# A decoder block in one program: lower-part terms last in the first half products, a turning step moved, an output split in front of two merges, the last tile by column halves

## The chip, the cores and the metric

The kernel runs on one core of a Trainium2 chip, and computes the whole block in one launch. The metric is the device time of that launch in microseconds. A run's time is one execution; the time of the kernel is the median of its runs.

## The reference

One decoder layer on 1024 tokens of width 1024, all in float32 (`rms_norm(x, g) = x * rsqrt(mean(x^2) + 1e-6) * g`):

```python
h = x
h = h + 0.5 * swiglu(rms_norm(h, ffn1_norm), ffn1_w1, ffn1_w3, ffn1_w2)   # 1024 -> 2816 -> 1024
u = rms_norm(h, mix_norm)
q, k, v, pz, gate_logits = split(u @ w_in)                 # 768, 768, 768, 512, 2 x 1024 columns
gates = sigmoid(gate_logits)
# 12 heads of 64, in 3 groups of 4 with (window, dilation) = (128,1), (512,4), (2048,16)
y_attn = dilated_mixture_attention(q, k, v) @ w_branch_attn
y_pool = multiscale_pool(pz, pool_w, pool_scale) @ w_branch_pool
merged = gates[:, :, 0] * y_attn + gates[:, :, 1] * y_pool
h = h + merged @ w_out
h = h + 0.5 * swiglu(rms_norm(h, ffn2_norm), ffn2_w1, ffn2_w3, ffn2_w2)
return rms_norm(h, final_norm)
```

In the attention the three groups of a head slot are added with weights that come of their softmax denominators.

## The kernel before

**Products.** Every operand of a large product is split into two parts: an upper part in the matmul's reduced float32 type (ScalarE copies it, names with `hi`) and a lower part, the operand less the upper one (VectorE or GpSimd subtracts, names with `lo`). A product of blocks is then three matmuls: upper by upper, upper by lower, lower by upper. The function `three` lists them in that order. The large products are also made in seven block products instead of eight, on sums and differences of halves; the table `DOWN` says for each of the seven which halves of the result it is added to and with which sign. A matmul writes 128 rows and up to 512 columns of one PSUM bank.

**Order.** The program runs under a manual schedule: each engine works its instructions in the order in which the code issues them, and waits only for what it reads or overwrites. SP issues most transfers, in one queue; ScalarE issues a few.

**The first products.** `run_first(n, ks, terms)` multiplies the first block of the first up-projections: `u_first0` for w1 and `u_first1` for w3, over four slices `k` of the width, with the activations' parts `xhi`, `xlo`. The slices 2 and 3 come later than 0 and 1, since their activations are loaded later; VectorE makes their `xlo`.

**The attention.** `scores(q)`, `masked`, `exponents`, `trans_p` (transposes, `tp`), `split_p` (`ehi` on ScalarE, `elo` on VectorE) and `values(q)` (products `o`) run as a pipeline over `q`, with `house(s)` behind each step for what is due at step `s`, and the pool branch's products `yp` as `fill`. `make_factors` is a generator: each `advance(factors[0])` does its next part. Its third part for the first half of the heads, the turning step, transposes the factors `f` on TensorE (`f_turned`), copies them on ScalarE and stores them (`f_by_head`), and the next part loads them spread over rows (`f_of`). In `house` the parts are advanced at the steps `N // 2 + 8` to `N // 2 + 12`.

**The output product.** `merge(k)` for `k` from 0 to 15 multiplies a column block of the attention branch (six matmuls into a bank, `ya{k}`), multiplies it with the gate on VectorE (`merge{k}`), and adds the pool branch on GpSimd (`merged`). The banks of the tag `mm` are four, so that `ya6` takes that of `ya2`. `sum_o(0)` and `split_o(0)` split the first two blocks of the merged operand: `o_hi0` on ScalarE and `o_lo0` on VectorE, each in two halves. `step_o(0)` then multiplies them with the output weights (`wo`).

**The last product.** `Down.run` ends with a loop over four tiles `t` of 128 rows: the tile's last matmuls (`multiply`, nine of 128x512 into one bank), `add` on VectorE to the residual `h`, and `after2`, which makes the final norm: squares summed on ScalarE (`high_half`), a power on GpSimd (`power`), and `send_out`, in which VectorE scales the upper columns and ScalarE the lower ones and both are stored, 128x512 each. `send_out(3 + t)` of one tile stands behind `high_half` of the next.

## Time and profile before

| | us |
|---|---|
| median of 3 runs | 1876.7 |
| lowest and highest of them | 1875.4, 1876.83 |
| the profiled execution | 1877.42 |
| its span | 1875.2 |
| TensorE busy in the span | 1863.7 (99%) |
| VectorE busy | 1366.2 (73%) |
| GpSimd busy | 783.9 (42%) |
| ScalarE busy | 768.4 (41%) |

The span is what the profile covers, from the first instruction to the end. The granted TensorE clock is 0.999 of full speed over it. TensorE's busy time is nearly the whole span, so the table to read beside it is what TensorE waits for, and what follows its last matmul.

### The profile page before, as it was taken

How to read it: one execution, taken by the hardware profiler on the slowest of the kernel's cores; microseconds unless marked ns; L12 is line 12 of the kernel's file. 1: busy time of each engine (PE TensorE's matmuls, PEld its weight loads, DVE VectorE, ACT ScalarE, POOL GpSimd, SP SyncE). 2: the span in 40 equal slices, each digit the busy share in tenths (PEclk: the TensorE clock that was granted, in tenths of full speed). 3: DMA queues.
4: the chain of work that ended last, by engine and by line, in shares of the span. 5: the costliest groups of instructions: out<-in, count | busy, mean ns of one | idle time of the engine just before them, and what ended most of it. 6: DMA issues, size and time to landing. Idle time of an engine off the chain costs nothing.

```text
span 1875.2 us, 24419 instructions
## 1 busy us (share of the span) xinstructions
PE 1863.7 (99%) x8667; PEld 1545.1 (82%) x8667; DVE 1366.2 (73%) x1966; ACT 768.4 (41%) x1393; POOL 783.9 (42%) x569
## 2 busy tenths in 40 slices
PE   9999999999999999999999999999999999999998
PEld 8888888888888888888888887888888888888886
DVE  7887866668886776658885886887765566577867
ACT  7422323233345643334445772463333333343344
POOL 5554644452222364445554467544333333312221
PEclk9999999999999999999999999999999999999999
DMA  8134324356565436765578888634332233354654
GB/s 327 45 124 149 121 95 152 117 206 209 192 231 198 157 114 208 258 211 185 213 251 324 314 254 298 267 129 180 120 139 85 90 107 122 126 203 157 223 197 146
DMA packets 148369, 339.70 MB, mean 181 GB/s; under 512 B 18024, under 2 KB 39576, under 8 KB 146712
## 3 DMA queue, kind: packets, MB, share of 16 engines
q1 hardware_dynamic: 144504, 327.30, 50.1%
q10 hardware_dynamic: 3744, 10.85, 1.6%
q8 instruction: 68, 1.11, 0.2%
q14 instruction: 53, 0.43, 0.1%
HBM read 237.48 MB, written 100.62 MB: 180 GB/s over the span
## 4 chain that ended last, share of the span: by engine, by line
PE 55%; DVE 2%; ACT 2%; DMA 1%; issue 1%; POOL 1%; SPq 0%; ACTq 0%; POOLq 0%; DVEq 0%
PE u_mixm L334 15%; PE d_f L904 8%; PE wo L2368 4%; PE yp L2110 2%; PE o L2048 1%; PE u_f20a L334 1%; PE u_f20b L334 1%; PE u_f21b L334 1%; PE u_f21a L334 1%; PE u_f210b L334 1%; PE u_f210a L334 1%; PE u_f29b L334 1%; PE u_f29a L334 1%; PE u_f28b L334 1%; PE u_f28a L334 1%; PE u_f27b L334 1%
## 5 line engine op out<-in xcount | busy, mean ns | idle before, releaser
L904 PE MATMUL d_f<-bhi_f,ahi_f 128*128 128x512 f32 x616 | 240.2, 390 | 0.0
L904 PE MATMUL d_f<-bhi_f,alo_f 128*128 128x512 f32 x616 | 239.8, 389 | 0.0
L904 PE MATMUL d_f<-blo_f,ahi_f 128*128 128x512 f32 x616 | 239.7, 389 | 0.0
L861 POOL TENSOR_TENSOR alo_f<-g_f,ahi_f 128x512 fp32r<-128x512 f32 x60 | 86.7, 1462 | 269.0 <-ACT ahi_f L857 269.0
L334 PE MATMUL u_mixm<-xhi_t_mix,wc_mixm 128*128 128x512 f32 x608 | 157.3, 391 | 0.1
L904 PEld LDWEIGHTS d_f<-bhi_f,alo_f 128*128 128x128 f32 x616 | 115.6, 188 | 24.3 <-DVE alo_f L861 0.2
L904 PEld LDWEIGHTS d_f<-bhi_f,ahi_f 128*128 128x128 f32 x616 | 115.6, 188 | 24.1 <-ACT h L424 0.5
L904 PEld LDWEIGHTS d_f<-blo_f,ahi_f 128*128 128x128 f32 x616 | 115.7, 188 | 24.0
L334 PEld LDWEIGHTS u_mixm<-xhi_t_mix,wc_mixm 128*128 128x128 f32 x608 | 113.5, 188 | 23.8 <-ACT wc_mixm L322 0.5
L334 PE MATMUL u_mixm<-xhi_b_mix,wc_mixm 128*128 128x512 f32 x456 | 120.3, 391 | 0.0
L325 POOL TENSOR_TENSOR wc_mixm<-s_mixm,wc_mixm 128x512 fp32r<-128x512 f32 x52 | 77.1, 1483 | 101.8 <-ACT wc_mixm L322 95.7
L334 PEld LDWEIGHTS u_mixm<-xhi_b_mix,wc_mixm 128*128 128x128 f32 x456 | 84.9, 188 | 17.2
L322 ACT ACTIVATE wc_mixm<-s_mixm 128x512 fp32r<-128x512 f32 x76 | 47.0, 628 | 111.4 <-DVE s_mixm L378 56.4
L857 ACT ACTIVATE ahi_f<-g_f 128x1024 fp32r<-128x1024 f32 x84 | 81.9, 975 | 6.8 <-DMA g_f<-gs_f 6.6
L334 PE MATMUL u_mixm<-xlo_t_mix,wc_mixm 128*128 128x512 f32 x304 | 81.3, 389 | 0.0
L325 POOL TENSOR_TENSOR wc_mixm<-raw,wc_mixm 128x512 fp32r<-128x512 f32 x41 | 62.3, 1522 | 37.9 <-ACT wc_mixm L322 24.6
L2368 PE MATMUL wo<-w_o,o_hi 128*128 128x512 f32 x224 | 69.4, 391 | 0.0
L646 POOL TENSOR_TENSOR y_f<-y_f,norm_ffn 128x512 f32<-128x512 f32 x35 | 54.4, 1560 | 35.5 <-DVE y_f L627 25.2
L857 ACT ACTIVATE bhi_f<-s_f2w 128x512 fp32r<-128x512 f32 x55 | 32.9, 627 | 86.0 <-DVE s_f2w L879 69.6
L857 ACT ACTIVATE bhi_f<-s_f1w 128x512 fp32r<-128x512 f32 x55 | 33.1, 629 | 83.5 <-DVE s_f1w L879 70.8
L334 PEld LDWEIGHTS u_mixm<-xlo_t_mix,wc_mixm 128*128 128x128 f32 x304 | 57.1, 188 | 12.0
L861 DVE TENSOR_TENSOR alo_f<-g_f,ahi_f 128x1024 fp32r<-128x1024 f32 (+1 forms) x48 | 58.6, 1222 | 7.7 <-ACT ahi_f L857 7.7
(1360 smaller groups left out, 4823.4 us busy)
## 6 DMA issues: line engine op xcount, KB each, us to landing
g_f<-gs_f SPq DMA_DIRECT2D x70, 512.0 KB
gs_f<-y_f SPq DMA_DIRECT2D x88, 256.0 KB
raw<-in_w2a_dram SPq DMA_DIRECT2D x35, 512.0 KB
raw<-in_w2b_dram SPq DMA_DIRECT2D x35, 512.0 KB
gs_f<-gb_f SPq DMA_DIRECT2D x46, 256.0 KB
raw<-in_w1b_dram SPq DMA_DIRECT2D x22, 512.0 KB
raw<-in_w3b_dram SPq DMA_DIRECT2D x22, 512.0 KB
raw<-in_w1a_dram SPq DMA_DIRECT2D x20, 512.0 KB
```

What stands on the lines that cost most here:

```text
L322: ac.activation(w[:, 0], src, AF.Copy)
L325: eng.tensor_tensor(w[:, 1], src, w[:, 0].bitcast(F32), op=OP.subtract)
L334: pe.matmul(p, a, b, start=(start and n == 0), stop=(n == 11), skip_group_check=not start)
L646: gp.tensor_tensor(c, c, self.sv.norm[:, cols], op=OP.mult)
L857: ac.activation(hi[:, c], src, AF.Copy)
L861: eng.tensor_tensor(lo[:, d], src[:, o], hi[:, d].bitcast(F32), op=OP.subtract)
L904: pe.matmul(self.banks[m][t], l, r, start=(first and q == 0), stop=(last and q == 2))
L2048: pe.matmul(p, l, r, start=(j == 0), stop=(j == end))
L2110: pe.matmul(p, a, b, start=(j == 0), stop=(j == 11))
L2368: pe.matmul(banks[m][t], l, r, start=(st == 0 and j == 0 and q == 0), stop=(st == 1 and j == 1 and q == 2))
```

## The change

Four places in the code are edited.

1. In the first products the slices 2 and 3 of `u_first0` and `u_first1` were each done whole (upper parts, then lower). Now the terms with the activations' upper part are done for both, then those with the lower part for both.
2. The turning step is advanced no longer in `house` but inside step `q`, behind the transposes and the `fill` of that step and in front of `values(q - 2)`.
3. `sum_o(0)` and `split_o(0)` are issued behind `merge(1)` instead of `merge(3)`; `sum_o(1)` stays.
4. The fourth tile of the last product is multiplied, added and squared in two halves of 256 columns. Its first half is issued in `after2` of the third tile. The fourth tile's two sums of squares are added into one on VectorE. The stores of the lower columns of the tiles 5 and 6 go into SP's queue instead of ScalarE's.

```diff
-        def multiply(self, i, t):
+        def multiply(self, i, t, c=slice(0, HALF)):
...
-                for q, (l, r) in enumerate(three(tuple(v[:, j, ts] for v in a), tuple(v[:, j, :] for v in w))):
-                    pe.matmul(self.banks[m][t], l, r, start=(first and q == 0), stop=(last and q == 2))
-
-        def add(self, m, t):
+                for q, (l, r) in enumerate(three(tuple(v[:, j, ts] for v in a), tuple(v[:, j, c] for v in w))):
+                    pe.matmul(self.banks[m][t][:, c], l, r, start=(first and q == 0), stop=(last and q == 2),
+                              skip_group_check=c.start > 0)
...
+        def last_half(self, m, b, part):
+            c, i = (slice(0, HALF // 2), slice(HALF // 2, HALF))[b], len(self.steps) - 1
+            self.multiply(i - 1, 3, c)
+            self.multiply(i, 3, c)
+            self.add(m, 3, c)
+            part(b, c)
...
-                        self.multiply(i - 1, t)
-                        self.multiply(i, t)
-                        self.add(m, t)
+                        if part and t == 3:
+                            self.last_half(m, 1, part)
+                        else:
+                            self.multiply(i - 1, t)
+                            self.multiply(i, t)
+                            self.add(m, t)
                         after(m, t)
...
-        run_first(0, (2, 3), (0, 2, 1))
-        run_first(1, (2, 3), (0, 2, 1))
+        for terms in ((0, 2), (1,)):
+            for n in (0, 1):
+                run_first(n, (2, 3), terms)
...
-        if s - N // 2 in (8, 9, 10, 11, 12):
+        if s - N // 2 in (8, 9, 10, 12):
             advance(factors[0])
...
+                if 2 * q == N // 2 + 12:
+                    advance(factors[0])
             if q > 1:
                 values(q - 2)
...
+            if k == 1:
+                sum_o(0)
+                split_o(0)
             if k == 3:
-                sum_o(0)
                 sum_o(1)
-                split_o(0)
...
+    def last_part(b, c):
+        y, st = ends[7]
+        c = slice(HALF + c.start, HALF + c.stop)
+        ac.activation(y[:, c], h[7][:, c], AF.Square, scale=D ** -0.5, accum_out=st[:, (4, 2)[b]:(5, 3)[b]])
+        if b == 0:
+            ve.tensor_tensor(st[:, 0:1], st[:, 0:1], st[:, 4:5], op=OP.add)
+
     def high_half(t):
+        if t == 7:
+            return
...
-            nc.scalar.dma_start(out[rows, LOWS], y[:, LOWS])
+            (nc.scalar if t == 7 else nc.sync).dma_start(out[rows, LOWS], y[:, LOWS])
...
+            if t == 3:
+                power(7)
             if t > 0:
                 send_out(3 + t)
-            power(4 + t)
+            if t == 2:
+                down.last_half(m, 0, last_part)
+            if t < 3:
+                power(4 + t)
```

**How it moves instructions.** The rows that follow say the line, the operation, what it writes and from what, the shape, and in brackets the engines or queues that it waits for (ending in `_49`, `DMAHW` for transfers); "x2" stands for two alike.

TensorE at the turning step, before: the last value products `o15`, the transposition, and the first scores of the next step.

```order
L2048 MATMUL o15_9731<-ehi15_9690,v4_0_in_9319 128x256
L2048 MATMUL o15_9731<-elo15_9691,v4_0_in_9319 128x256
L2048 MATMUL o15_9731<-ehi15_9690,v4_1_in_9320 128x256
L1917 MATMUL f_turned_9767<-ident_72,f0_9702 48x128 [waits Pool_49]
L1968 MATMUL s18_0_9773<-qk5_1_hi_9429,qk5_0_hi_9426 128x128
L1968 MATMUL s18_1_9774<-qk5_1_hi_9429,qk5_0_hi_9426 128x128 [waits DVE_49]
```

TensorE at the turning step, after: the end of the pool branch's fill `yp10`, the transposition, and the value products `o16` of the next step.

```order
L2122 MATMUL yp10_9722<-xhi_t2_mix_5437,wab5_9489 128x512
L2122 MATMUL yp10_9722<-xlo_t2_mix_5438,wab5_9489 128x512 x3
L1929 MATMUL f_turned_9805<-ident_72,f0_9702 48x128 [waits DVE_49,Pool_49]
L2060 MATMUL o16_9810<-ehi16_9749,v5_0_in_9570 128x256 [waits DMAHW5_49]
L2060 MATMUL o16_9810<-elo16_9750,v5_0_in_9570 128x256
L2060 MATMUL o16_9810<-ehi16_9749,v5_1_in_9571 128x256 [waits DMAHW6_49]
```

The transposition has moved behind a whole step of scores, transposes and fill, in front of `o16`; `o15` and `s18` now follow on each other.

VectorE at the output product's start, before: the last product of the attention (`att`), two merges, the lower parts of the first split, two merges.

```order
L2091 TENSOR_TENSOR att1_1_10274<-o1_2_9869,att1_0_10273 128x512 [waits Activation_49]
L2178 TENSOR_TENSOR merge2_10277<-merge2_10277,ya2_10404 128x512 [waits DMAHW4_49,DMAHW2_49,PE_49]
L2178 TENSOR_TENSOR merge3_10308<-merge3_10308,ya3_10418 128x512 [waits DMAHW5_49,PE_49]
L2356 TENSOR_TENSOR o_lo0_10431<-merged0_0_10387,o_hi0_10430 128x512 [waits Activation_49] x2
L2178 TENSOR_TENSOR merge4_10311<-merge4_10311,ya4_10438 128x512 [waits DMAHW7_49,PE_49]
L2178 TENSOR_TENSOR merge5_10389<-merge5_10389,ya5_10453 128x512 [waits DMAHW4_49,DMAHW1_49,PE_49]
```

VectorE at the same place, after.

```order
L2103 TENSOR_TENSOR att1_1_10274<-o1_2_9869,att1_0_10273 128x512 [waits Activation_49]
L2370 TENSOR_TENSOR o_lo0_10405<-merged0_0_10387,o_hi0_10404 128x512 [waits Activation_49] x2
L2190 TENSOR_TENSOR merge2_10277<-merge2_10277,ya2_10410 128x512 [waits DMAHW4_49,DMAHW2_49,PE_49]
L2190 TENSOR_TENSOR merge3_10308<-merge3_10308,ya3_10424 128x512 [waits DMAHW5_49,PE_49]
L2190 TENSOR_TENSOR merge4_10311<-merge4_10311,ya4_10438 128x512 [waits DMAHW7_49,PE_49]
L2190 TENSOR_TENSOR merge5_10389<-merge5_10389,ya5_10453 128x512 [waits DMAHW4_49,DMAHW1_49,PE_49]
```

The two `o_lo0` have moved in front of `merge2` and `merge3`.

VectorE in the tail, before: the additions of the third and fourth tile (`h6_last`, `h7_last`), the statistics (`nst`) and the scalings (`n4`).

```order
L912 SCALAR_TENSOR_TENSOR h6_last_14054<-d_f26_2_15994,h6_last_14054 128x512 [waits PE_49]
L2560 SCALAR_TENSOR_TENSOR n4_5_16081<-h5_last_14052,nst_last5_16082,gain_final_14058 128x512 [waits Pool_49]
L2554 SCALAR_TENSOR_TENSOR nst_last6_16127<-nst_last6_16127 128x1 [waits Activation_49]
L912 SCALAR_TENSOR_TENSOR h7_last_14056<-d_f26_3_15995,h7_last_14056 128x512 [waits PE_49]
L2560 SCALAR_TENSOR_TENSOR n4_6_16126<-h6_last_14054,nst_last6_16127,gain_final_14058 128x512 [waits Pool_49]
L2554 SCALAR_TENSOR_TENSOR nst_last7_16168<-nst_last7_16168 128x1 [waits Activation_49]
L2560 SCALAR_TENSOR_TENSOR n4_7_16167<-h7_last_14056,nst_last7_16168,gain_final_14058 128x512 [waits Pool_49]
```

VectorE in the tail, after.

```order
L913 SCALAR_TENSOR_TENSOR h6_last_14054<-d_f26_2_15994,h6_last_14054 128x512 [waits PE_49]
L2584 SCALAR_TENSOR_TENSOR n4_5_16081<-h5_last_14052,nst_last5_16082,gain_final_14058 128x512 [waits Pool_49]
L913 SCALAR_TENSOR_TENSOR h7_last_14056<-d_f26_3_15995,h7_last_14056 128x256 [waits PE_49]
L2568 TENSOR_TENSOR nst_last7_16168<-nst_last7_16168 128x1 [waits Activation_49]
L2578 SCALAR_TENSOR_TENSOR nst_last6_16127<-nst_last6_16127 128x1
L913 SCALAR_TENSOR_TENSOR h7_last_14056<-d_f26_3_15995,h7_last_14056 128x256 [waits PE_49]
L2578 SCALAR_TENSOR_TENSOR nst_last7_16168<-nst_last7_16168 128x1 [waits Activation_49]
L2584 SCALAR_TENSOR_TENSOR n4_6_16126<-h6_last_14054,nst_last6_16127,gain_final_14058 128x512 [waits Pool_49]
L2584 SCALAR_TENSOR_TENSOR n4_7_16167<-h7_last_14056,nst_last7_16168,gain_final_14058 128x512 [waits Pool_49]
```

The addition of the fourth tile is two of 256 columns, its first stands in front of the third tile's statistics, and the scaling of `n4_6` has moved behind the second. On TensorE the nine last matmuls are now eighteen of 256 columns, of which the tenth waits for VectorE, as the rows around it show:

```order
L904 MATMUL d_f26_3_15995<-bhi_f240_16114,alo_f240_16121 128x256
L904 MATMUL d_f26_3_15995<-bhi_f241_16157,ahi_f241_16161 128x256
L904 MATMUL d_f26_3_15995<-blo_f241_16158,ahi_f241_16161 128x256
L904 MATMUL d_f26_3_15995<-bhi_f241_16157,alo_f241_16162 128x256
L904 MATMUL d_f26_3_15995<-bhi_f240_16114,ahi_f240_16120 128x256 [waits DVE_49]
L904 MATMUL d_f26_3_15995<-blo_f240_16115,ahi_f240_16120 128x256
L904 MATMUL d_f26_3_15995<-bhi_f240_16114,alo_f240_16121 128x256
```

What has moved there: the second half of the columns starts anew with the first weights, in the same bank.

## Rows read from the trace of the kernel before

**Rows 1.** Busy times by stretch: us, busy us of each engine (x instructions), TensorE clock.

```profile
1866.00:1875.20 9.20, 2.27 (x11) 1.54 (x9) 4.43 (x9) 3.39 (x7) 2.09 (x3) 0.74 0.62 228
...
sum 1875.20, PE 1863.74 PEld 1545.12 DVE 1366.21 ACT 768.36 POOL 783.90; mean PE 931.87 PEld 772.56 DVE 683.10 ACT 384.18 POOL 391.95
```

**Rows 2.** Timeline of TensorE, first products: start, us, instruction, [idle before <- releaser].

```profile
10.38 0.39 PE L1158 MATMUL u_first<-xlo_b_f,wc_first 128*128 128x512 f32 x1
11.75 0.50 PE L1158 MATMUL u_first<-xlo_b_f,wc_first 128*128 128x512 f32 x1 [0.98 <-DVE xlo_b_f L1066]
12.09 1.10 PE L1158 MATMUL u_first<-xhi_b_f,wc_first 128*128 128x512 f32 x4
13.03 0.62 PE L1158 MATMUL u_first<-xlo_b_f,wc_first 128*128 128x512 f32 x2
```

**Rows 3.** Timeline of GpSimd, first products.

```profile
6.25 3.12 POOL L1148 TENSOR_TENSOR wc_first<-raw,wc_first 128x256 fp32r<-128x256 f32 x4 [5.81 <-ACT wc_first L1144]
```

**Rows 4.** Timeline of TensorE around the turning step.

```profile
1095.18 0.28 PE L2048 MATMUL o<-elo,v_in 128*128 128x256 f32 x1
1095.30 0.28 PE L2048 MATMUL o<-ehi,v_in 128*128 128x256 f32 x1
1096.20 0.29 PE L1917 MATMUL f_turned<-ident,f 128*48 128x128 f32 x1 [0.62 <-POOL f L1912]
1096.43 0.33 PE L1968 MATMUL s<-qk_hi,qk_hi 64*128 64x128 f32 x2
...
1099.33 0.28 PE L2048 MATMUL o<-ehi,v_in 128*128 128x256 f32 x1
...
1100.96 1.26 PE L2015 MATMUL tp<-ident,e 128*128 128x128 f32 x4
```

**Rows 5.** Timeline of ScalarE around the turning step.

```profile
1096.53 0.27 ACT L1919 ACTIVATE f_turned<-f_turned 48x128 f32<-48x128 f32 x1 [1.70 <-PE f_turned L1917]
1098.67 0.60 ACT L2027 ACTIVATE ehi<-tp 128x512 fp32r<-128x512 f32 x1 [1.86 <-PE tp L2015]
1099.16 1.15 ACT L1590 ACTIVATE xlo_b_mix<-xhi_b_mix 128x512 fp32r<-128x512 f32 x2
```

**Rows 6.** Timeline of VectorE at the output product's start.

```profile
1138.90 0.68 DVE L2178 TENSOR_TENSOR merge<-merge,ya 128x512 f32<-128x512 f32 x1
1141.65 0.69 DVE L2178 TENSOR_TENSOR merge<-merge,ya 128x512 f32<-128x512 f32 x1 [2.08 <-DMA merge<-gate]
1142.26 2.37 DVE L2356 TENSOR_TENSOR o_lo<-merged,o_hi 128x512 fp32r<-128x512 f32 x2
```

**Rows 7.** Timelines of TensorE, ScalarE and GpSimd at the output product's start.

```profile
1139.17 3.34 PE L2176 MATMUL ya<-att,ya 128*128 128x512 f32 x14
...
1144.68 0.50 PE L2368 MATMUL wo<-w_o,o_lo 128*128 128x512 f32 x1 [0.72 <-DVE o_lo L2356]
...
1145.02 0.64 PE L2368 MATMUL wo<-w_o,o_hi 128*128 128x512 f32 x2
...
1140.16 0.63 ACT L2355 ACTIVATE o_hi<-merged 128x512 fp32r<-128x512 f32 x1 [1.07 <-POOL merged L2182]
...
1136.62 4.75 POOL L2182 TENSOR_TENSOR merged<-merge 128x512 f32<-128x512 f32 x3
```

**Rows 8.** Timeline of the tail, from the last matmuls to the last store.

```profile
1867.24 0.74 DVE L2560 SCALAR_TENSOR_TENSOR n<-h_last,nst_last,gain_final 128x512 f32<-128x512 f32 x1
...
1867.89 0.39 PE L904 MATMUL d_f<-bhi_f,alo_f 128*128 128x512 f32 x1
...
1868.31 0.69 DVE L912 SCALAR_TENSOR_TENSOR h_last<-d_f,h_last 128x512 f32<-128x512 f32 x1
...
1871.62 0.34 ACTq L2565 DMA_DIRECT2D out_dram<-n  x1
```

**Rows 9.** Groups of instructions by line and form: busy us, mean ns of one.

```profile
L2030 DVE TENSOR_TENSOR elo<-tp,ehi 128x256 fp32r<-128x256 f32 x10 | 4.2, 422 | 1.8 <-ACT ehi L2027 1.7
```

**Rows 10.** Transfers from 1871.6 us on, GB/s in 40 slices of 0.09 us.

```profile
GB/s 387 410 432 364 251 69 0 114 319 410 364 364 387 364 364 364 364 387 364 410 387 432 341 92 0 0 0 0 0 0 0 0 0 0 0 0 0 0 0 0
```

More of the change, by code (lines that the diff above doesn't have):

```diff
@@ L902, in multiply, with add @@
                 first, last = s == 0 and j == 0, s == len(PAIRS) - 1 and j == size - 1
-                for q, (l, r) in enumerate(three(tuple(v[:, j, ts] for v in a), tuple(v[:, j, :] for v in w))):
-                    pe.matmul(self.banks[m][t], l, r, start=(first and q == 0), stop=(last and q == 2))
-        def add(self, m, t):
+                for q, (l, r) in enumerate(three(tuple(v[:, j, ts] for v in a), tuple(v[:, j, c] for v in w))):
+                    pe.matmul(self.banks[m][t][:, c], l, r, start=(first and q == 0), stop=(last and q == 2),
+                              skip_group_check=c.start > 0)
+        def add(self, m, t, c=slice(0, HALF)):
             for (th, n), sign in DOWN[m].to:
-                hs = h[4 * th + t][:, n * HALF:(n + 1) * HALF]
+                hs = h[4 * th + t][:, n * HALF + c.start:n * HALF + c.stop]
                 by = 0.5 * sign
@@ L911, in add, with run @@
                     by = self.halves[sign][:, 4 * th + t:4 * th + t + 1]
-                ve.scalar_tensor_tensor(hs, self.banks[m][t], by, hs, op0=OP.mult, op1=OP.add)
-        def run(self, pool, after, tick=None):
+                ve.scalar_tensor_tensor(hs, self.banks[m][t][:, c], by, hs, op0=OP.mult, op1=OP.add)
+        def last_half(self, m, b, part):
[4 more added lines that the diff above has]
+            part(b, c)
+        def run(self, pool, after, tick=None, part=None):
             def half_tile(tag, n):
@@ L1157, in run_first @@
                     a, b = three((w[:, 0, r], w[:, 1, r]), (hi[:, k, :], lo[:, k, :]))[i]
-                    pe.matmul(banks[n], a, b, start=(k == 0 and i == 0), stop=(k == 3 and i == terms[-1]))
+                    pe.matmul(banks[n], a, b, start=(k == 0 and i == 0), stop=(k == 3 and i == 1))
         FRONT, BACK = slice(0, 2 * P), slice(2 * P, HALF)
@@ L2535, in low_half @@
     def low_half(t):
-        y, st = h_tile(f"n4_{t}"), small.tile([P, 4], F32, tag="nlast", name=f"nst_last{t}")
+        y, st = h_tile(f"n4_{t}"), small.tile([P, 5], F32, tag="nlast", name=f"nst_last{t}")
         ac.activation(y[:, LOWS], h[t][:, LOWS], AF.Square, scale=D ** -0.5, accum_out=st[:, 0:1])
@@ L2594, in tile_block @@
         with tc.manual_schedule():
-            down.run(pool, after2)
+            down.run(pool, after2, part=last_part)
     dstack.close()
```

## The prediction

> **What bounds the kernel now.** I read the busy times by stretch first. TensorE works 1863.7 of 1875.2 us [rows 1], so all that it waits for comes to 11.5 us, and 6.9 of these lie behind its last matmul, from 1866 us on, where it works 2.27 of 9.20 us. No edit can be worth more than the waits that it touches. 0.2% of the time, which is about what a measurement of this kernel can tell from no change, is 3.75 us. The list of waits by engine then says which line waits for whom, and timelines of four places give the rest; in those, a wait stands in brackets behind the row. The four edits touch four places, in order of time: a 0.98 us wait of TensorE for VectorE at 11.75 [rows 2]; a 0.62 us wait for GpSimd at 1096.20 [rows 4]; a 0.72 us wait for VectorE at 1144.68 [rows 7]; and the tail, in which no matmul is left and the time is that of one chain through VectorE, ScalarE, GpSimd and a store [rows 8]. The profiled execution took 1877.42 us, 2.2 more than its span, and 0.72 more than the median of the three runs, 1876.7. I make the sum as a difference and put it on the median.
>
> **Lower-part terms last.** TensorE has done the four upper-part matmuls of `u_first0` and starts its lower-part one at 10.38; the next needs a part that VectorE finishes only at 11.75. Behind it stand `u_first1`'s four upper-part matmuls at 12.09, which need nothing late: their rows show no wait [rows 2], and GpSimd has split the last of their weights by 6.25 + 3.12 = 9.37 [rows 3]. The change puts these four into the gap. They take 13.03 - 12.09 = 0.94, so they fill 10.38 to 11.32; the first lower-part matmul takes until about 11.55, the second still waits for 11.75, and all behind it comes 0.94 earlier: **-0.94**. What is left of the gap is 0.2. Bounds: -1.05 if the slow restart (the matmul at 11.75 takes 0.34 to the next, not 0.23) goes too, and 0 if a later wait for an operand swallows all. After that, up to the middle of the program, the list of waits has for TensorE none as long as this one; I take -0.94.
>
> **Turning step moved.** Before, TensorE starts its last `o15` matmul at 1095.30, the transposition `f_turned` waits for GpSimd until 1096.20, and the scores `s18` start at 1096.43. A matmul of 256 columns takes 0.12 to the next (1095.18 to 1095.30), so without the step the scores start at about 1095.42: 1.01 earlier [rows 4]. The step itself comes behind the fills, in front of `o16`, which stood at 1099.33, so at about 1098.32; GpSimd is long done by then. But the change leaves ScalarE's order alone: its copy of `f_turned` still stands in front of `ehi17`. The copy started 0.33 after the transposition, so now at 1098.65, and takes 0.27; `ehi17`, at 1098.67 before, starts at about 1098.89, and ScalarE then works without a pause through two splits and four exponentials [rows 5], which `tp18` on TensorE waits for: four matmuls from 1100.96 take 1.26 [rows 4]. So TensorE gains 1.01 and gives it back at `tp18`, where it is ScalarE's 0.22 that counts: **+0.2**. Bounds: -0.9 if ScalarE's lateness does not reach `tp18`; +0.9 if the step's two transfers, on SP's queue now behind the store of `by_pool4` and 2.1 us later (copy at 1098.65, not 1096.53), hold up the factors that GpSimd and VectorE multiply with. In the waits of this stretch TensorE waits for nothing that comes of those factors before the branch products, 30 us on, so I take the ScalarE number.
>
> **First split in front of two merges.** Before, VectorE does `merge2` at 1138.90, waits for a load until 1141.65, does `merge3`, and only at 1142.26 the two `o_lo` of the first split, 2.37 for both [rows 6]: 0.69 for one, as `merge3` shows for the size, and 1.7 for the other. TensorE waits for it at 1144.68 for 0.72, and goes on with its seventh `wo` matmul at 1145.02 [rows 7]. A matmul of 512 columns takes (3.34 - 0.39) / 13 = 0.227 (the 14 of `ya`), so this is as if `wo` had started at 1145.02 - 6 x 0.227 = 1143.66 without a wait. After, the first `o_lo` goes while GpSimd makes the second of its additions (three take it from 1136.62 to 1141.37 now; ScalarE's second `o_hi` waits for the second until 1140.16). The second `o_lo` comes behind that `o_hi`, 1140.16 + 0.63 = 1140.79, and takes 0.69, to 1141.48: GpSimd's third addition needs `merge2`, and so stands still then. Then comes `merge2`, until 1142.15 and not 1139.58. That is a new wait: `ya6` takes the bank that `merge2` reads, and would have started at 1139.17 + 8 x 0.227 = 1140.98. It starts at 1142.2, its six matmuls end at 1143.6, and `wo` then runs without a wait: 1143.6 against 1143.66, **-0.05**. Bounds: -1.1 if `ya6` is not held, and +1.0 if the second `o_lo` takes the 1.7 us that it takes now. `merge3` waits for its load until 1141.65 either way.
>
> **Last tile by halves.** Nine matmuls of 512 columns become eighteen of 256. The order shows a wait on VectorE at the first matmul of the second half: the addition of the first half reads the bank that the second half writes. The nine used to start at 1867.89 - 8 x 0.227 = 1866.07. Now half 0 ends at 1866.07 + 8 x 0.12 + 0.28 = 1867.31. Its addition finds VectorE in a row of 0.74 from 1867.24, so it starts at 1867.9 [rows 8], takes 0.42 (the one row type of 256 columns out of PSUM: 422 ns [rows 9]) and ends at 1868.32. Half 1 runs from 1868.37 to 1869.61, its addition starts at 1869.65. Before, the whole addition started at 1868.31. So 1.34 is lost, and the shorter addition (0.69 to 0.42) and a square shortened as much give 0.5 back: the last store would be issued +0.84 later, at 1872.46. That isn't all: `n4_6`'s scaling now stands behind the second addition and its statistics, so that four stores of 256 KB go out within a us, not two. In the last stretch bytes flow from 1872.2 to 1873.76 for two stores (17 slices of 0.09), 0.75 each, starting 0.6 behind the issue at 1871.62, and the span ends 1.44 later [rows 8, 10]. Four, the first issued at about 1871.5, flow from 1872.1 to 1875.1: 1.35 later than 1873.76, **+1.4** rounded up for the issues. Bounds: +0.84 if the stores cost nothing more, and +2.2 if additions and squares of half the width cost as much as whole ones and the stores come in addition. A bound below nothing belongs to the rival without the wait.
>
> The Trainium skill, "PSUM — Partial Sum Buffer", section "PSUM bank collisions raise a hardware error", says that two engines on one bank collide even at disjoint columns, and that the compiler makes any two such instructions depend on each other. By it the wait is there and the last edit is a loss, and without it that term would be -0.45; no row of before shows a bank shared by halves, and the order prints the wait. The same skill, "SBUF — State Buffer", section "The DMA setup-cost knee", gives a transfer 2 us and its bytes at 436 GB/s, by which I estimate two more stores of 256 KB at +1.2 instead of 1.4.
>
> **Sum.** -0.94 + 0.2 - 0.05 + 1.4 = +0.6, so 1876.7 + 0.6 = **1877.3**: no change that can be measured.
>
> **Rivals.** (1) *Each edit does what it removes.* -1.05, -0.9, -1.1, and in the tail a second half that does not wait: it ends at 1868.3 as before, and the shorter addition and square give -0.45. Together -3.5: 1873.2. For it speaks that each wait is in the trace, against it that rows 5 and 6 show what stands behind each of the last three. (2) *The stores at the end pile up*, the other side. Four stores drain together. At the 228 GB/s that the last stretch had on average [rows 1] the megabyte takes 4.6 us, so bytes flow until 1876.7, +2.9, and the sum gives 1878.8. Over +0.2% it comes below 170 GB/s (6.2 us: +4.5). Against it: the last slices show 341 to 432 GB/s. (3) *The early gain is swallowed* by a later wait for an operand that ScalarE or GpSimd makes at their own pace: 0 for the first edit, 1878.2.
>
> **How the numbers follow.** I give the forecast 0.6, rival 1 0.15, rival 2 0.13, rival 3 0.12. The likeliest's own range has the tail between +0.84 and +2.2 and half the spread of the three runs (1.4) either way: 1876.0 to 1878.8. To hold 8 in 10 the range goes down to 1874.5, where the first three edits do what rival 1 says and the tail loses its least (-3.05 + 0.84 = -2.2), and up to 1880.2: rival 2 with the upper bound of the turning step (+0.7) and half the spread. Faster by over 0.2% needs more than all of rival 1, and holds 0.06. Slower by over 0.2% needs rival 2 at its point or several upper bounds: 0.08. The rest, 0.86, is within 0.2%.
>
> **What would show it.** Right: TensorE reaches `u_f11a` at about 12.55; `f_turned` stands without a wait near 1098.3 and `tp18` comes no earlier than before against the rows around it; `ya6` has a wait for `merge2` of about 1.2, and `wo` none for `o_lo`; a gap of about 1 us in front of the tenth of the last eighteen matmuls, and four stores in the last 4 us. Wrong: no gap at the tenth matmul or at `ya6` (then it is faster than said, by 1.3 each at most), or the 0.94 of the start gone by 60 us.

## The result, and the profile after

| | median us | runs | lowest to highest |
|---|---|---|---|
| before | 1876.71 | 20 | 1875.4 to 1879.13 |
| after | 1880.12 | 20 | 1879.15 to 1881.37 |

The ratio is 1.0017, with a 95% interval from 1.0011 to 1.0024: the change costs 3.4 us, and between 2.1 and 4.5 by the interval. The time lies inside the range, by 0.1, and inside 0.2% (3.75 us), 2.8 above the forecast time. The interval lies above 1, so there is a change, and its upper end lies past 0.2% and past the range. The profiled execution took 1880.36 us with a span of 1878.1.

The waits of TensorE in the changed kernel (engine, line, what it waited for: us in total, times, longest):

```profile
PE fa L1958 <- ACT f_of L1949: 1.1, 1, 1.1
PE idle L1052 <- DVE fours L1053: 1.1, 1, 1.1
PE ya L2188 <- DVE merge L2190: 1.0, 1, 1.0
PE d_f L904 <- DVE h_last L913: 1.0, 1, 1.0
PE tp L2027 <- ACT e L2007: 0.8, 2, 0.6
PE d_f L904 <- POOL alo_f L861: 0.5, 1, 0.5
```

Of the three waits on which the prediction was built, those for `xlo` [rows 2], `f` [rows 4] and `o_lo` [rows 7], none is left. Four of 0.5 to 1.1 us stand in their place: `fa`, `ya`, the `d_f` for VectorE and that for GpSimd. The third and fourth line, `ya` and `d_f <- h_last`, were forecast with about their sizes (1.2 and 1). The first was not forecast. The line of `tp`, of which 0.6 is the wait at `tp18`, was.

The last stretch, which answers to [rows 1]:

```profile
1866.00:1878.10 12.10, 4.10 (x26) 3.42 (x24) 5.79 (x13) 4.31 (x11) 2.83 (x4) 0.78 0.47 173
```

TensorE works 4.10 of its 12.10 us, not 2.27 of 9.20: the end of the third tile and the eighteen matmuls, with a wait between them. TensorE at the start, which answers to [rows 2]:

```profile
9.66 1.87 PE L1169 MATMUL u_first<-xhi_b_f,wc_first 128*128 128x512 f32 x7
11.37 1.07 PE L1169 MATMUL u_first<-xlo_b_f,wc_first 128*128 128x512 f32 x4
12.27 1.07 PE L334 MATMUL u_f11a<-xhi_b_f,wc_f11a 128*128 128x512 f32 x4
```

The seven upper-part and four lower-part matmuls run without a gap. The four lower-part ones run from 11.37 on, where [rows 2] had the last two at 13.03, and `u_f11a` behind them starts at 12.27; before it started at 13.49. From the last tile's first matmul to the end of the span it was 1875.2 - 1866.07 = 9.1; now it is 1878.1 - 1867.53 = 10.6.

The turning step and what hangs on it, in the order of the chain, after (TensorE's rows at the step first, then SP's queue, GpSimd, ScalarE, TensorE):

```profile
1098.28 0.28 PE L1929 MATMUL f_turned<-ident,f 128*48 128x128 f32 x1
1100.83 1.48 PE L2027 MATMUL tp<-ident,e 128*128 128x128 f32 x4 [0.63 <-ACT e L2007]
...
1098.89 0.33 SPq L1932 DMA_DIRECT2D f_by_head<-f_turned  x1
...
1107.50 2.55 POOL L2093 TENSOR_TENSOR o<-o,f_of 128x512 f32<-128x512 f32 x2 [1.43 <-DMA f_of<-f_by_head]
...
1122.60 0.63 ACT L2102 ACTIVATE att<-o 128x512 fp32r<-128x512 f32 x1 [1.55 <-POOL o L2097]
1126.21 2.00 ACT L1949 ACTIVATE f_of<-f 128x1024 f32<-128x1024 f32 x2 [1.87 <-DVE f L1924]
...
1127.32 0.66 PE L1958 MATMUL fa<-ident,f_of 128*128 128x128 f32 x4 [1.06 <-ACT f_of L1949]
```

The store of the factors starts at 1098.89, not 1096.83. GpSimd's first product with the loaded factors comes at 1107.50 and waits 1.43 for their load; before it had no wait. GpSimd's products and sums follow on each other from there with one short pause, and ScalarE's copy `att` of the second round of them waits 1.55 for GpSimd at 1122.60; behind it in ScalarE's order stand two `ehi`, the exponent of the other half's factors, and at 1126.21 the copies that spread them (`f_of`). TensorE's transpositions `fa` of these wait until 1127.32. The first two rows show the step itself as it was forecast: no wait at 1098.28, and 0.63 for ScalarE at `tp18`. In the kernel before GpSimd, `att` and `fa` had no wait in the same chain:

```profile
1096.83 0.33 SPq L1920 DMA_DIRECT2D f_by_head<-f_turned  x1
...
1105.94 2.56 POOL L2081 TENSOR_TENSOR o<-o,f_of 128x512 f32<-128x512 f32 x2
...
1121.06 0.63 ACT L2090 ACTIVATE att<-o 128x512 fp32r<-128x512 f32 x1
1124.69 2.00 ACT L1937 ACTIVATE f_of<-f 128x1024 f32<-128x1024 f32 x2 [1.89 <-DVE f L1912]
...
1126.03 0.60 PE L1946 MATMUL fa<-ident,f_of 128*128 128x128 f32 x4
```

The output product, TensorE and VectorE, and the tail, in the timelines of after (answering to [rows 6, 7, 8]):

```profile
1143.68 1.66 PE L2188 MATMUL ya<-att,ya 128*128 128x512 f32 x6 [1.04 <-DVE merge L2190]
1145.17 0.62 PE L2382 MATMUL wo<-w_o,o_hi 128*128 128x512 f32 x2
...
1140.64 2.39 DVE L2370 TENSOR_TENSOR o_lo<-merged,o_hi 128x512 fp32r<-128x512 f32 x2
1142.94 2.56 DVE L2190 TENSOR_TENSOR merge<-merge,ya 128x512 f32<-128x512 f32 x4
...
1867.53 0.28 PE L904 MATMUL d_f<-bhi_f,ahi_f 128*128 128x256 f32 x1
...
1869.28 0.42 DVE L913 SCALAR_TENSOR_TENSOR h_last<-d_f,h_last 128x256 f32<-128x256 f32 x1
...
1869.75 0.39 PE L904 MATMUL d_f<-bhi_f,ahi_f 128*128 128x256 f32 x1 [0.99 <-DVE h_last L913]
...
1871.13 0.42 DVE L913 SCALAR_TENSOR_TENSOR h_last<-d_f,h_last 128x256 f32<-128x256 f32 x1 [0.39 <-PE d_f L904]
...
1874.14 0.37 ACTq L2589 DMA_DIRECT2D out_dram<-n  x1
```

`ya6` waits 1.04 for `merge2`, which starts at 1142.94 behind the two `o_lo`, and `wo` then runs without a wait. In the tail the first half's addition starts at 1869.28, the tenth matmul waits 0.99 for it, and the last issue on ScalarE's queue comes at 1874.14, 6.6 behind the tile's first matmul; before it was 5.55 (1866.07 to 1871.62).

Laid side by side, the two traces say where the 2.9 us between their spans come from. TensorE in the changed kernel is 1.2 ahead at `u_f11a` (12.27 against 13.49), 0.1 ahead at the last `o15` (1095.16 against 1095.30), 1.3 behind at `fa` (1127.32 against 1126.03), 1.5 behind from the output product to the last tile (1867.53 against 1866.07) and 2.9 behind at the end. So the start's gain is lost before the turning step, the turning step costs 1.4 up to `fa`, the split next to nothing and the tail 1.4. Each trace is one execution.

### The profile page after: what moved, and what is told of

Its sections match the earlier page's. It is cut to its first block, busy times and chain, and to the rows that moved or that the text cites. A ratio compares the mean times of both kernels' runs of the same rounds, so it can differ in the third digit from the quotient of the medians.

```text
span 1878.1 us, 24443 instructions
## 1 busy us (share of the span) xinstructions
PE 1864.4 (99%) x8676; PEld 1545.2 (82%) x8676; DVE 1368.2 (73%) x1968; ACT 768.1 (41%) x1395; POOL 783.1 (42%) x569
## 4 chain that ended last, share of the span: by engine, by line
PE 53%; DVE 2%; ACT 2%; POOL 1%; issue 1%; DMA 1%; SPq 0%; POOLq 0%; ACTq 0%; DVEq 0%
PE u_mixm L334 15%; PE d_f L904 8%; PE wo L2382 4%; PE yp L2122 1%; PE u_f20a L334 1%; PE u_f21b L334 1%; PE u_f20b L334 1%; PE u_f21a L334 1%; PE u_f210b L334 1%; PE u_f210a L334 1%; PE u_f29b L334 1%; PE u_f29a L334 1%; PE u_f28b L334 1%; PE u_f28a L334 1%; PE u_f27b L334 1%
```

## The experiments

Each kernel was timed against the kernel before on the same chip, 11 runs of it and 33 of before. The differences are of medians, the intervals those of the ratio, each about 1.7 us wide to either side. Nothing is left out of the computation in any of them.

| kernel | us against before | ratio, 95% interval |
|---|---|---|
| a_only | -0.36 | 0.9999 (0.9990 to 1.0008) |
| b_only | +1.03 | 1.0007 (0.9998 to 1.0016) |
| c_only | -0.05 | 1.0001 (0.9992 to 1.0010) |
| d_only | +1.66 | 1.0009 (1.0001 to 1.0018) |
| b_swap | +4.13 | 1.0023 (1.0014 to 1.0032) |
| late_store | +2.17 | 1.0014 (1.0005 to 1.0023) |
| b_early | +2.12 | 1.0010 (1.0001 to 1.0018) |
| c_two | -0.46 | 0.9997 (0.9988 to 1.0006) |
| d_bank | +0.55 | 1.0005 (0.9996 to 1.0013) |
| d_acts | +1.21 | 1.0009 (1.0000 to 1.0017) |
| a_c_two | -0.12 | 0.9997 (0.9988 to 1.0006) |
| best | +0.52 | 1.0002 (0.9993 to 1.0011) |

**Each edit alone.** The kernel before with one edit of the diff above.

> The kernel before with the first edit alone (lower-part terms last in the first half products). Theory 1, from the trace after the change: TensorE is 0.9 to 1.2 us ahead from 13 us on, but at about 464 us it waits for GpSimd's lower part of a reloaded operand, whose transfer does not come earlier by as much, and at 760 us for ScalarE once more; some 0.2 is left at 1090 us, so the time is -0.2 (within +-0.6) against before. Theory 2, the prediction: nothing swallows it, -0.94. The start itself should show no wait of 0.98 for the lower part under either.

> The kernel before with the second edit alone (turning step moved). Theory 1: the step's late transfers cost, not its place on TensorE: the loads of the factors start some 2.1 us later, the row statistics of the other half of the heads, behind them in SP's queue, land some 2 us later, VectorE waits for them near 1121, and TensorE waits about 1.1 us for the spread factors at its transpositions near 1126: +1.4 to +1.6 in all, with the 0.2 of ScalarE at tp18. Theory 2, the prediction: only ScalarE's 0.2 at tp18 counts: +0.2. Theory 3: the stall near 1126 comes of another edit in front of it (the first one's shift); then it is absent here and the time is +0.2 too, with no wait of VectorE for the statistics.

> The kernel before with the third edit alone (first split in front of two merges). Theory 1 and the prediction: the wait moves from the wo matmuls to ya6, which is held by about 1.2 us for merge2, and the net is 0 (-0.1 to +0.1). Rival: ya6 is held in the changed kernel because all there is 1.5 us late; alone the edit gains the 1.1 us of the two waits for o_lo, -1.1.

> The kernel before with the fourth edit alone (last tile by column halves, two stores moved to the other queue). Theory 1 and the prediction: TensorE stands about 1 us in front of the tenth of the eighteen last matmuls, the last store is issued 0.9 to 1.1 later against the first matmul of the last tile, and the time is +1.4 (1.2 to 1.7). Rival: the loss belongs to what came in late from the edits in front, and alone the halves cost nothing or gain: 0 to -0.45.

The four add up to +2.3, under the +3.4 of all together but within its interval (2.1 to 4.5); whether the 1.1 between them is more than the spread stays open. By these intervals only the fourth edit is told from 0, and it costs; that the second costs too rests on its trace and on the kernels that follow. The first is worth little and the third nothing that could be measured.

*The first edit.* The 0.98 us that it takes away is not in every execution. Each kernel's trace is one execution. Of the ten traces of kernels without the edit, the list of waits has TensorE waiting for VectorE's `xlo` in five, but in two of these at another place:

| before | b_only | c_two | b_early | d_acts | c_only, d_only, b_swap, late_store, d_bank |
|---|---|---|---|---|---|
| 1.0 | 1.1 | 1.0 | 0.7 | 0.7 | none |

The 0.7 of `b_early` and `d_acts` stands in front of the first two slices, which the edit leaves alone; at the slices 2 and 3 these traces have no wait:

```profile
7.95 0.50 PE L1158 MATMUL u_first<-xlo_b_f,wc_first 128*128 128x512 f32 x1 [0.65 <-DVE xlo_b_f L1066]
```

So the wait of [rows 2] is there in three traces of ten, which is 0.31 in the mean, and -0.36 is what the edit alone gave. VectorE and GpSimd show why, first in the kernel before, then in `a_only`, whose edit does not touch their order, and in `c_only`; the second row of the first two is the second lower part alone:

```profile
8.68 3.01 DVE L1066 SCALAR_TENSOR_TENSOR xlo_b_f<-x_t,gain,xhi_b_f 128x512 fp32r<-128x512 f32 x2 [2.00 <-ACT xhi_b_f L1057]
...
9.84 1.85 DVE L1066 SCALAR_TENSOR_TENSOR xlo_b_f<-x_t,gain,xhi_b_f 128x512 fp32r<-128x512 f32 x1
...
9.86 1.28 POOL L325 TENSOR_TENSOR wc_f11a<-raw,wc_f11a 128x512 fp32r<-128x512 f32 x1 [0.49 <-ACT wc_f11a L322]
```

```profile
8.88 1.79 DVE L1066 SCALAR_TENSOR_TENSOR xlo_b_f<-x_t,gain,xhi_b_f 128x512 fp32r<-128x512 f32 x2 [1.41 <-ACT xhi_b_f L1057]
...
9.93 0.74 DVE L1066 SCALAR_TENSOR_TENSOR xlo_b_f<-x_t,gain,xhi_b_f 128x512 fp32r<-128x512 f32 x1
...
10.06 1.77 POOL L325 TENSOR_TENSOR wc_f11a<-raw,wc_f11a 128x512 fp32r<-128x512 f32 x1 [0.59 <-ACT wc_f11a L322]
```

```profile
8.59 1.84 DVE L1066 SCALAR_TENSOR_TENSOR xlo_b_f<-x_t,gain,xhi_b_f 128x512 fp32r<-128x512 f32 x2 [1.37 <-ACT xhi_b_f L1057]
```

Two lower parts took VectorE 1.79 and 1.84 where the second of them started ahead of GpSimd's subtraction, and 3.01 in the kernel before, where the second one took 1.85 and not 0.74; there GpSimd's took 1.28, and in `a_only` 1.77. The ten traces without the edit fall apart in the same way. In the three with the wait GpSimd's subtraction took 1.28 to 1.33 and VectorE's 1.77 to 1.85; in the seven others, GpSimd's took 1.74 to 1.83 and VectorE's 0.74 or 1.23. In these seven VectorE started 0.06 to 0.64 us ahead; in `b_only` and `c_two` GpSimd was 0.1 ahead (9.87 against 9.97, 10.27 against 10.38), and in the kernel before the two starts lie 0.02 apart (9.84 and 9.86). Which of the two is stretched hangs on a tenth or less. The Trainium skill, "SBUF — State Buffer", section "SBUF: two separate sides", says that a VectorE operation with two inputs in SBUF and a GpSimd operation that reads SBUF take one pair of ports as an exclusive lock, whoever starts first for the whole instruction; the nine traces with starts at least 0.06 apart agree, and that of the kernel before cannot tell who was first.

In the profile of the changed kernel the early gain was mostly gone by the turning step: the last `o15` came at 1095.16, 0.14 ahead of [rows 4], after a new wait of 0.5 for GpSimd's `alo_f` at 464 us and smaller losses near 727 and 760 us. In the traces of `a_only` and `c_only` a start that was earlier by a us stayed so up to the output product, so swallowing it is not the rule; this part of the first theory fell.

*The second edit.* `b_only` shows the chain again, with a wait for the statistics that was expected:

```profile
1099.24 0.33 SPq L1920 DMA_DIRECT2D f_by_head<-f_turned  x1
...
1107.92 2.55 POOL L2081 TENSOR_TENSOR o<-o,f_of 128x512 f32<-128x512 f32 x2 [1.50 <-DMA f_of<-f_by_head]
...
1123.02 0.63 ACT L2090 ACTIVATE att<-o 128x512 fp32r<-128x512 f32 x1 [1.62 <-POOL o L2085]
...
1122.86 0.17 DVE L1903 TENSOR_TENSOR top<-top,stats 128x16 f32<-128x16 f32 x1 [1.22 <-DMA stats<-st]
...
1127.75 0.66 PE L1946 MATMUL fa<-ident,f_of 128*128 128x128 f32 x4 [1.14 <-ACT f_of L1937]
```

VectorE waits 1.22 for the statistics at 1122.86, but what VectorE makes of them goes to ScalarE's exponent, which stands behind `att` and two `ehi`, so this trace does not yet tell which of the two sets the end. The next two kernels do.

**The transfers or the place.** `late_store` leaves the transposition and its copy where they were, and makes the transfers late, at the price of a second small copy on ScalarE:

```diff
             ac.activation(turned, p, AF.Copy)
-            nc.sync.dma_start(f_dram.rearrange("g a i p -> (g a i) p"), turned)
+            yield
+            again = att_small.tile([GROUPS * 2 * NT, P], F32, name="f_turned_again")
+            ac.activation(again, turned, AF.Copy)
+            nc.sync.dma_start(f_dram.rearrange("g a i p -> (g a i) p"), again)
...
                 advance(splits[q - 1], 2)
+            if 2 * q == N // 2 + 12:
+                advance(factors[0])
```

> The kernel before, in which the turning step stays where it was on TensorE and ScalarE, but what is stored is a second copy, which ScalarE makes behind ehi17, so that the store and the four loads of the factors start some 2.6 us later (2.1 in the changed kernel). Theory 1 (late transfers): VectorE waits for the statistics near 1121 and TensorE for the spread factors near 1126, 1.1 to 1.7 us, with the f_turned wait of 0.6 still there: +1.2 to +1.8. Rival (place): the cost of the second edit is what the step does at its new place on TensorE and ScalarE; then this costs only the copy, +0.3 or less.

It cost 2.17, with the transposition at its old place: late transfers cost by themselves. In its trace GpSimd waits 2.75 for the factors and `fa` 1.24, and the eight `tp` in front of that take 1.91, before 1.04:

```profile
1095.33 0.29 PE L1917 MATMUL f_turned<-ident,f 128*48 128x128 f32 x1 [0.62 <-POOL f L1912]
...
1108.05 2.55 POOL L2084 TENSOR_TENSOR o<-o,f_of 128x512 f32<-128x512 f32 x2 [2.75 <-DMA f_of<-f_by_head]
...
1116.76 1.91 PE L2018 MATMUL tp<-ident,e 128*128 128x128 f32 x8
...
1127.84 0.66 PE L1949 MATMUL fa<-ident,f_of 128*128 128x128 f32 x4 [1.24 <-ACT f_of L1940]
```

It does not match the second edit in size. Its loads are issued 6.6 us behind the last `o15` (1094.43 to 1101.04), in `b_only` 5.2 (1095.51 to 1100.71), in the kernel before 3.0 (1095.30 to 1098.31), so they are later than the edit makes them; that goes with the larger cost.

`b_swap` puts what stands behind the factors' loads in SP's queue in front of them:

```diff
-        if s - N // 2 in (8, 9, 10, 12):
+        if s - N // 2 in (8, 9, 10):
             advance(factors[0])
         if i == 4 and u + 1 < len(uses):
             load_values(uses[u + 1])
         if u > 0 and i == 4 and slots[s - 5][1] != 0:
             get_stats(*slots[s - 5][:2])
+        if s - N // 2 == 12:
+            advance(factors[0])
```

> The second edit alone, with one thing more: in SP's queue the loads of the next values and the statistics of the other half of the heads stand in front of the four loads of the factors, so that they fill the time in which the transfers wait for the late turning step (about 5 us without a byte in the changed kernel's trace, 1097.2 to 1102.2). Theory 1 (late transfers): the statistics come back to where they were or earlier, VectorE's wait for them near 1121 and TensorE's 1.1 us at the transpositions near 1126 go, and +0.2 of ScalarE at tp18 is left: +0.0 to +0.3 against before, some 1 us under the edit alone. Rival: the lateness comes of the factors themselves, not of what is queued behind them; then GpSimd, which needs them near 1106, is later still by some 2 us, and the time is +1.0 or more.

It cost 4.13, four times the edit alone. So the theory that the statistics behind the loads set the end fell: with them out of the way the loads of the factors themselves came later, and GpSimd waited 3.75 for them:

```profile
1109.38 1.30 POOL L2081 TENSOR_TENSOR o<-o,f_of 128x512 f32<-128x512 f32 x1 [3.75 <-DMA f_of<-f_by_head]
...
1118.09 1.91 PE L2015 MATMUL tp<-ident,e 128*128 128x128 f32 x8 [1.05 <-ACT e L1995]
...
1129.18 0.66 PE L1946 MATMUL fa<-ident,f_of 128*128 128x128 f32 x4 [1.25 <-ACT f_of L1937]
```

ScalarE's `att` waits for GpSimd, and since its exponents for the attention stand behind it, `tp` waits too, 1.05, and then `fa`, 1.25. The chain is: store of the turned factors, their load, GpSimd's products, ScalarE in order, `fa`.

**The step one place earlier.** `b_early` advances the step behind `scores(q + 1)` in place of behind the fill:

```diff
                 scores(q)
                 scores(q + 1)
+            if 2 * q == N // 2 + 12:
+                advance(factors[0])
```

> The second edit with the turning step one place earlier: behind the scores s18 and s19, in front of the transposes tp17, where GpSimd's factors are there and ScalarE is idle. Theory 2 (chain of the factors): the loads are there 8.7 us after the store starts (1099.24 to 1107.92 in the kernel with the second edit alone), GpSimd then multiplies, ScalarE copies and makes the exponent of the other half's factors behind that, and TensorE's transpositions near 1126 come at the end with 0.2 to spare before. The store is some 0.7 later than before, so GpSimd starts some 0.2 later, and what TensorE gains at 1096 it gives back near 1126: 0.0 (-0.3 to +0.4). Rival (wait on TensorE): the 0.6 wait was worth something, nothing here is late enough to count: -0.6 to -0.9.

```profile
1097.21 0.27 PE L1917 MATMUL f_turned<-ident,f 128*48 128x128 f32 x1 [0.72 <-DVE own_stats L1986]
...
1106.38 2.55 POOL L2081 TENSOR_TENSOR o<-o,f_of 128x512 f32<-128x512 f32 x2 [1.05 <-DMA f_of<-f_by_head]
...
1126.23 0.66 PE L1946 MATMUL fa<-ident,f_of 128*128 128x128 f32 x4 [0.70 <-ACT f_of L1937]
```

The forecast of a store 0.7 later was wrong: the transposition takes a bank of the four that the scores use, and waited 0.72 for VectorE to read it. The load came late here too, GpSimd waited 1.05 and `fa` 0.70. The time, +2.12, is more than these waits explain in this trace, whose execution at 1876.99 was one of the fastest three of its kernel; the rest stays open. Neither place that was tried behind the old one gained.

**The split one merge later.** As the third edit, with `if k == 2` for `if k == 1`.

> The third edit alone with the split one merge later, behind merge(2): VectorE does merge2, both lower parts, merge3. Theory: what holds ya6 is merge2 behind the lower parts; with merge2 in front, ya6 starts with no wait near its 1140.98 of before, the lower parts end by about 1142, before wo needs them, and the time is -0.9 to -1.2 against executions with the whole o_lo wait, -0.4 to -0.8 on the median, since that wait was short in some executions. Rival: merge3, now behind the lower parts, holds the next product's bank and the wait only moves on: 0.

```profile
1138.67 5.15 PE L2176 MATMUL ya<-att,ya 128*128 128x512 f32 x22
1143.65 0.62 PE L2368 MATMUL wo<-w_o,o_hi 128*128 128x512 f32 x2
1144.11 0.39 PE L2368 MATMUL wo<-w_o,o_lo 128*128 128x512 f32 x1
```

The 22 `ya` matmuls and `wo` run through without a wait, in 5.15 us: neither `ya6` nor `wo` is held, which the theory said and the rival denied. (`fa` waits 0.4 in this trace, though the turning step is at its old place.) The gain of -0.46 has 0 in its interval.

The 0.72 of [rows 7] is a sample too. Of the nine traces with the split behind `merge(3)`, the list has a wait for `o_lo` in three (0.7 in the kernel before, 0.2 in `b_only`, 1.0 in two waits in `late_store`) and none in six, while `ya6` waits 1.04 in both traces with the split behind `merge(1)`. By these traces the third edit should lose that us against an execution without the old wait; why the median of `c_only` shows no loss stays open.

**The halves of the last tile.** In `d_bank` the second half goes into a bank of its own; the first addition takes the whole first bank, and the sums of squares are added behind the second one:

```diff
-                    pe.matmul(self.banks[m][t][:, c], l, r, start=(first and q == 0), stop=(last and q == 2),
-                              skip_group_check=c.start > 0)
+                    p = self.rest if c.start > 0 else self.banks[m][t]
+                    begin = c.start > 0 and i == len(self.steps) - 2 and j == 0
+                    end = self.name == "f2" and t == 3 and i == len(self.steps) - 3 and j == size - 1
+                    pe.matmul(p[:, c], l, r, start=((first or begin) and q == 0), stop=((last or end) and q == 2),
+                              skip_group_check=c.start > 0 or c.stop < HALF)
...
-            self.add(m, 3, c)
+            self.add(m, 3, c if b else slice(0, HALF))
```

> The fourth edit alone, with the second half of the columns multiplied into a bank of its own (the first addition takes the whole first bank, so the sum of the earlier steps too; the two sums of squares are added behind the second addition). Theory 1 (shared bank): the gap of 1 us in front of the tenth matmul is gone, additions and squares in halves end about when the whole ones did, and +0.1 to +0.5 is left, of the stores of two lower parts on the other queue. Rival (stores): the loss of 1.4 is the four stores close together; then +1.0 or more is left.

In `d_acts` the lower parts' stores of tiles 5 and 6 go back to ScalarE's queue (`nc.scalar.dma_start` for all).

> The fourth edit alone, with the lower parts' stores of all three tiles on ScalarE's queue, as before. Theory 1: of the loss, 0.85 is the shared bank (10.63 from the last tile's first matmul to the end with the edit, 9.76 with a bank of its own, 9.1 to 9.7 without the edit) and some 0.4 the four stores close together; the other queue does not change when the scaled rows are ready, so a part of the 0.4 at most goes: +1.1 to +1.4 against before. Rival (queue): SP's queue, in which the stores stand in order, makes them late: +0.9 or less.

```profile
1864.07 0.28 PE L907 MATMUL d_f<-bhi_f,ahi_f 128*128 128x256 f32 x1
...
1865.02 0.28 PE L907 MATMUL d_f<-bhi_f,alo_f 128*128 128x256 f32 x1
...
1865.14 0.28 PE L907 MATMUL d_rest<-bhi_f,ahi_f 128*128 128x256 f32 x1
```

With a bank of its own the tenth matmul, `d_rest`, follows on the ninth at the same 0.12. From the tile's first matmul to the end of the span it is 1873.8 - 1864.07 = 9.7 us, and with the shared bank 10.7 in `d_only` (1864.73 to 1875.4) and 10.7 in `d_acts` (1864.32 to 1875.0); without the edit it is 9.1 in the kernel before, 9.2 in `c_only` and 9.7 in `b_only`, the longest. So of the edit's 1.4 the wait for the shared bank is 0.9 to 1.0. The rest is small: +0.55 has 0 in its interval. From the last issue to the end it is 3.6 in the kernel before and in `b_only` (1871.62 to 1875.2, 1873.21 to 1876.8), and some 3.9 with the four stores close together in the changed kernel and in `d_bank` (1874.17 to 1878.1, 1869.85 to 1873.8). By the Trainium skill, "PSUM — Partial Sum Buffer", section "PSUM bank collisions raise a hardware error", two engines must not touch one bank at the same time, at disjoint columns either. The traces agree in so far as the program waits, 1.01 in one bank (`d_only`) and not at all in two (`d_bank`); no run here shows a collision. SP's queue for two more stores is hardly the cause of the rest: with the other queue the tail takes as long, though its wait in front of the tenth matmul was 1.17 against 1.01, so that a tenth or two may be the queue's.

**The pieces that did not lose, together.** `a_c_two` has the first edit and the split behind `merge(2)`, `best` these and the step behind the scores.

> The first edit and the split behind merge(2), which were -0.4 and -0.5 alone, both within their intervals of 0. Theory: both waits are there in some executions only (a lower part by VectorE beside a subtraction by GpSimd), and the edits take them away where they are; the two add up, -0.8 (-0.4 to -1.2). Rival: both were noise: 0.

> The first edit, the split behind merge(2) and the turning step behind the scores, without the halves of the last tile. Theory 2 (chain of the factors): the turning step adds nothing to the two others: -0.8 (-0.4 to -1.2). Rival (wait on TensorE): -1.4 to -1.8.

`a_c_two`, at -0.12 with 1876.29, cannot be told from the kernel before; neither theory is shown by it. `best` is 0.6 above it, within the intervals, but in its trace `f_turned` waits 0.7 for VectorE and `fa` 0.5 for ScalarE, as in `b_early`. No version beat the kernel before by more than its interval.

## Why the prediction was right and where it was off

The time, 1880.1, was inside the range, and the ratio stayed within 0.2%. That is luck in part. The likeliest's own range ended at 1878.8. The upper end of the whole range, 1880.2, was rival 2 with the turning step's upper bound and half the spread: the turning step did come out near that bound, but the stores of rival 2 did not pile up. "No change that can be measured" was wrong too: with 20 runs of each, the interval begins at 1.0011. The forecast of +0.6 against +3.4 is off by terms, as follows.

- **Lower-part terms last, -0.94 forecast, -0.36 measured alone.** The mechanism was right: the gap of [rows 2] is gone. The size was read from one execution, and its wait is there in three traces of ten only.
- **Turning step, +0.2 forecast, +1.0 measured alone.** The gain on TensorE and its return at `tp18` came as said: `f_turned` stands without a wait at 1098.28 and `tp18` waits 0.63 for ScalarE. What failed is the step with which the +0.9 for the late transfers was put aside: that TensorE waits for nothing that comes of the factors before the branch products. It waited for nothing before because the chain ended just in time; with the transfers 2.1 later, `fa` waits 1.06. From the kernel with the edit, the factors are there 8.7 after their store starts (1099.24 to 1107.92); from 1096.83 that is 1105.5, 0.4 before GpSimd came to them. `fa` comes 1.1 behind ScalarE's first copy (1126.21 to 1127.32), before 1.3 (1124.69 to 1126.03), so 0.2 to spare there. The cover was some 0.2 to 0.4 us, an estimate from these rows, and the step's transfers came 2.1 later. It is not there in every execution: in `d_only`, with the step at its old place, the factors took 9.7 (1095.99 to 1105.66) and GpSimd waited 0.52 for them.
- **First split, -0.05 forecast, -0.05 measured alone.** The wait moved from `wo` to `ya6`, 1.04 us, as worked out. That the old wait is in three traces of nine only was not in the sum, so the equal number is partly luck.
- **Last tile, +1.4 forecast, +1.66 measured alone, +1.4 in the trace** (10.6 against 9.1). The wait in front of the tenth matmul was 0.99. The division was a bit off: 1.05 of it is the later last issue (6.6 against 5.55), where 0.84 was said, and 0.4 the stores, where 0.55 was said. The 9.1 of the kernel before is the shortest of the ten traces without the edit, 9.1 to 9.7.

The four terms measured alone leave 1.1 of the 3.4 over. In the changed kernel's trace the start's gain is lost and the turning step costs 1.4, both worse than alone, but whether that is the rule is not shown.

Of the rivals, the third came true in the changed kernel's trace, where a wait for GpSimd's `alo_f` swallowed a good part of the early gain; in `a_only` it did not. The first fell in the last three places, and the stores did not pile up (rival 2).

## What to carry to other kernels

A wait that stands on a chain through a store and a load is not idle time to be filled: before moving its head, follow what it issues to the next engine that reads it, and measure how early that is there now; a view that lists waits shows nothing of a chain that ends a few tenths of a us in time. A wait read from one execution is a sample: where two engines can be stretched by each other, look at several traces before counting it, and at the place of the wait in each. Splitting a tile by columns inside one bank makes the next matmuls wait for the reader of the first half.

## What was not expected of the hardware

Who comes first by a tenth or less between VectorE and GpSimd decides which is stretched, and the same subtraction then took 0.74 or 1.85 us on the one, or 1.28 or 1.77 on the other. From the issue of the small store of the factors (24 KB) to the end of the wait for the first part of what is loaded from it, 8.3 us pass in `best` (1097.31 to 1105.61), 8.7 in `b_only` and 9.7 in `d_only`; the four loads hold 1.5 MB. In the changed kernel bytes flow at 16 GB/s in the first 1.5 us of this time and at 25 GB/s in the next 1.8, and at 189 to 223 GB/s then.
